# A quarter of the tokens leaves the dense expert products of a product-key layer: gathered rows and VectorE in their place

## The chip, the cores and the metric

One core of a Trainium2 chip runs the whole program in one launch. The metric is device microseconds of that core, as the median of the runs shown. TensorE (PE) multiplies, with weight loads (PEld) beside the products; VectorE (DVE), ScalarE (ACT) and GpSimd (POOL) work element by element; SyncE (SP) issues most transfers, GpSimd some.

## The reference

256 tokens of width 2048 pass a first block (a convolution and a state-space branch, then a product-key expert layer) and then two more layers. The change lies in the expert layer. Each token picks 16 experts for each of 8 heads out of 128 x 128 = 16384; expert e is a row of `u_tab` and a row of `v_tab`, both of 2048 numbers.

```python
def peer(h, w_q, sub_keys, u_tab, v_tab):
    """h: (B,S,D) -> (B,S,D). Product-key retrieval of single-neuron experts."""
    bsz, seq, d = h.shape
    tokens = h.reshape(bsz * seq // PEER_TOKEN_BLOCK, PEER_TOKEN_BLOCK, d)

    def block(xb):
        q = (xb @ w_q).reshape(PEER_TOKEN_BLOCK, PEER_HEADS, 2, PEER_HALF)
        s = jnp.einsum('thcd,hcnd->thcn', q, sub_keys).astype(jnp.float32)
        s_top, i_top = lax.top_k(s, PEER_TOPK)
        cand = s_top[:, :, 0, :, None] + s_top[:, :, 1, None, :]
        cand_idx = i_top[:, :, 0, :, None] * PEER_KEYS + i_top[:, :, 1, None, :]
        cand = cand.reshape(PEER_TOKEN_BLOCK, PEER_HEADS, PEER_TOPK * PEER_TOPK)
        cand_idx = cand_idx.reshape(PEER_TOKEN_BLOCK, PEER_HEADS, PEER_TOPK * PEER_TOPK)
        best, pos = lax.top_k(cand, PEER_TOPK)
        expert = jnp.take_along_axis(cand_idx, pos, axis=-1)
        gates = jax.nn.softmax(best, axis=-1).astype(xb.dtype)
        u_sel = u_tab[expert]
        v_sel = v_tab[expert]
        act = jax.nn.gelu(jnp.einsum('td,thkd->thk', xb, u_sel))
        return jnp.einsum('thk,thkd->td', gates * act, v_sel)

    out = lax.map(block, tokens)
    return out.reshape(bsz, seq, d)
```

The rest of the program (convolution, scan, gated delta rule, band attention, the large projections) keeps its operations.

## The kernel before

All data is float32. A product on TensorE runs in two or three passes on rounded parts: a number is split into a high part (`h`) and the rest (`l`). For every strip of weights, `strips` fetches a `raw` tile of 128 x 1024 by SP (`fetch`, L150), ScalarE makes its high part (`wh`, L162) and VectorE the rest (`wl`, L163), both into a ring that holds two such tiles; `raw` has three buffers. `self.width` says how many columns one L162 or L163 instruction takes: 1024 in the first block up to the experts, 512 from the experts to the end of the program.

The expert layer is computed densely, without looking which experts were picked.

- **`experts_in`.** After the queries (16 products with `peer_w_q`), 128 blocks follow, one for each 128 experts (the number c). A block has two `raw` tiles, thus 16 pieces of the contraction; for each piece `dual` issues a matmul of 512 columns (L175: `wh` times high and low part of 256 tokens) and one of 256 (L176: `wl` times the high part). `fold` (L181, L182) adds the two halves, L797 scales, and gelu goes to the activations `w` on ScalarE (L801, L803).
- **Top-k and gates.** During blocks 0 to 31 VectorE finds the picks (`topk`, two steps a block). After block 31 `gates` turns each token's picks into a 128 x 128 gate matrix: three VectorE instructions per token (`oj`, L942 and L944), two small matmuls (L954), and for eight tokens at a time a product into `w` (L966, L968). `GRATE` sets how many steps of it are issued in a piece of the contraction.
- **`experts_out`.** For each pair of experts c, c+1 and each of four groups of 512 output columns (first three groups, then the last), the activations are split (`ah`, `al`, L1009, L1010) and multiplied with a strip of `peer_v`: per expert three matmuls of 512 columns for each half of the tokens, six in all (L1018 to L1020). `finish` transposes the sums, adds the residual and hands on.

The program is written with generators (`Side`) whose steps are spread over the loops; a scheduler then orders each engine's instructions, by priorities and its own estimates. What stands in the built program is fixed: an engine takes its instructions in that order, and an instruction that waits holds up all behind it.

## Time and profile before

| | before |
|---|---|
| runs | 3355.83 us median of 3 (3353.45 to 3359.02) |
| profiled execution | 3351.08 us, span 3349.3 us |
| busy in the span | PE 3291.0, DVE 2667.1, ACT 2021.3, POOL 171.6 us |
| moved by DMA | 584.49 MB, mean 175 GB/s |
| granted TensorE clock, mean | 0.996 |

A row of a view names the line, the engine, the operation, and output and inputs by the program's names with their shapes (partitions x elements). The modelled length of a matmul runs over the start of the next, so the pace of TensorE is read from starts, not from lengths. VectorE's instructions overlap a little as well: what one costs behind another is the distance of their starts.

### The profile page before, as it was taken

The numbers are of one execution on the slowest core, as the hardware profiler recorded it, in microseconds if no ns is written. First come the engines' busy times: TensorE is split into PE (matmuls) and PEld (weight loads), VectorE is DVE, ScalarE is ACT, GpSimd is POOL, SyncE is SP. The second block draws the span as 40 slices with busy tenths as digits, with TensorE's granted clock in tenths as the row PEclk, the third lists the DMA queues.
The fourth block names the chain that finished last, engine by engine and source line by source line (L and its number), as shares of the span: only waits on it lengthen the run. The fifth ranks groups of instructions, "written<-read, shape, count | busy, mean of one in ns | idle before, by whom it ended". The sixth has DMA issues, their size and how long they took to land.

```text
span 3349.3 us, 53879 instructions
## 1 busy us (share of the span) xinstructions
PE 3291.0 (98%) x17962; PEld 2780.5 (83%) x17962; DVE 2667.1 (80%) x6200; ACT 2021.3 (60%) x4529; POOL 171.6 (5%) x319
## 2 busy tenths in 40 slices
PE   8999999999999999999999999999999999999999
PEld 7787778888888888888888888778888888888888
DVE  8999987789999999996555556868888768666685
ACT  6577755555555555555555556767666666566664
POOL 1211110000000000000000000000222100000000
PEclk9999999999999999999999999999999999999999
DMA  6544345765556555555666666655443436655556
GB/s 210 160 143 139 133 127 188 216 193 178 187 183 179 180 177 182 177 182 183 193 194 195 193 192 198 209 183 171 143 138 117 145 105 211 198 177 176 173 171 181
DMA packets 167655, 584.49 MB, mean 175 GB/s; under 512 B 19184, under 2 KB 25616, under 8 KB 167120
## 3 DMA queue, kind: packets, MB, share of 16 engines
q1 hardware_dynamic: 165600, 574.94, 54.8%
q0 software_dynamic: 1776, 6.10, 0.6%
q8 instruction: 141, 2.31, 0.3%
q14 instruction: 138, 1.13, 0.1%
HBM read 573.88 MB, written 7.09 MB: 173 GB/s over the span
## 4 chain that ended last, share of the span: by engine, by line
PE 90%; DVE 5%; ACT 2%; issue 1%; DMA 1%; POOL 1%; SPq 0%; ACTq 0%; DVEq 0%; POOLq 0%
PE g L175 36%; PE g L176 18%; PE va L1018 7%; PE va L1019 7%; PE va L1020 7%; PE g L1609 3%; PE g L1610 3%; PE g L1608 3%; DVE wl L163 2%; PE ip L1345 1%; ACT wh L162 1%; PE yp L639 1%; PE wp L954 1%; PE cps L175 1%; PE bu L611 1%
## 5 line engine op out<-in xcount | busy, mean ns | idle before, releaser
L162 ACT CAST wh<-raw 128x512 fp32r<-128x512 f32 (+1 forms) x1920 | 1274.2, 664 | 1080.3 <-PE g L175 553.2
L163 DVE TENSOR_TENSOR wl<-raw,wh 128x512 fp32r<-128x512 f32 (+1 forms) x1920 | 1433.8, 748 | 589.6 <-ACT wh L162 571.8
L175 PE MATMUL g<-X,wh 128*128 128x512 f32 x4752 | 1707.7, 401 | 23.0 <-ACT wh L162 8.8
L176 PE MATMUL g<-X,wl 128*128 128x256 f32 x4752 | 1337.0, 281 | 2.3 <-DVE wl L163 2.2
L175 PEld LDWEIGHTS g<-X,wh 128*128 128x128 f32 x4752 | 894.3, 188 | 234.6 <-issue 10.8
L176 PEld LDWEIGHTS g<-X,wl 128*128 128x128 f32 x4752 | 898.0, 189 | 9.9 <-DVE wl L163 5.1
L1018 PE MATMUL va<-wh,ah 128*128 128x512 f32 x1024 | 398.4, 391 | 4.5 <-DVE gg L797 2.3
L1019 PE MATMUL va<-wh,al 128*128 128x512 f32 x1024 | 400.2, 391 | 0.3 <-DVE al L1010 0.3
L1020 PE MATMUL va<-wl,ah 128*128 128x512 f32 x1024 | 399.1, 390 | 0.0
L1018 PEld LDWEIGHTS va<-wh,ah 128*128 128x128 f32 x1024 | 191.7, 188 | 46.9 <-ACT ah L1009 7.5
L1019 PEld LDWEIGHTS va<-wh,al 128*128 128x128 f32 x1024 | 192.6, 188 | 43.3 <-DVE al L1010 3.3
L1020 PEld LDWEIGHTS va<-wl,ah 128*128 128x128 f32 x1024 | 192.7, 188 | 39.7
L175 PE MATMUL g<-xo,wh 128*128 128x512 f32 x512 | 179.6, 395 | 0.0
L182 DVE TENSOR_TENSOR g<-g,fold 128x256 f32<-128x256 f32 x377 | 159.8, 424 | 4.5 <-ACT fold L181 4.0
L1608 PE MATMUL g<-wh,X 128*128 128x512 f32 x384 | 151.9, 396 | 0.0
L1610 PE MATMUL g<-wl,X 128*128 128x512 f32 x384 | 150.5, 392 | 0.0
L1609 PE MATMUL g<-wh,X 128*128 128x512 f32 x384 | 150.1, 391 | 0.0
L181 ACT COPY fold<-g 128x256 f32<-128x256 f32 x377 | 138.2, 367 | 13.5 <-DVE g L182 7.7
L176 PE MATMUL g<-xo,wl 128*128 128x256 f32 x512 | 143.6, 280 | 0.0
L944 DVE TENSOR_SCALAR oj<-iota,ijg 128x128 f16<-128x128 f16 x512 | 142.6, 307 | 0.0
L175 PEld LDWEIGHTS g<-xo,wh 128*128 128x128 f32 x512 | 96.0, 187 | 22.8 <-DVE xo L1471 0.3
L1010 DVE TENSOR_TENSOR al<-w,ah 128x256 fp32r<-128x256 f32 x256 | 106.7, 418 | 0.9 <-ACT ah L1009 0.8
(478 smaller groups left out, 3577.0 us busy)
## 6 DMA issues: line engine op xcount, KB each, us to landing
raw<-peer_u SPq DMA_DIRECT2D x256, 512.0 KB, 3.5
raw<-peer_v SPq DMA_DIRECT2D x256, 512.0 KB, 3.5
raw<-a_w_in SPq DMA_DIRECT2D x128, 512.0 KB, 3.5
raw<-w_in SPq DMA_DIRECT2D x112, 512.0 KB, 3.5
raw<-b_w_t SPq DMA_DIRECT2D x96, 512.0 KB, 3.5
raw<-w_out SPq DMA_DIRECT2D x32, 512.0 KB, 4.3
raw<-peer_w_q SPq DMA_DIRECT2D x32, 512.0 KB, 3.5
raw<-a_w_out SPq DMA_DIRECT2D x32, 512.0 KB, 3.7
```

What stands on the lines that cost most here:

```text
L162: self.marks["A"] = nc.scalar.copy(wh[:, e], raw[:, e])
L163: self.marks["V"] = nc.vector.tensor_tensor(out=wl[:, e], in0=raw[:, e], in1=wh[:, e].bitcast(F32), op=ALU.subtract)
L175: nc.tensor.matmul(pf, lhsT=wh, rhs=hl, start=start, stop=False)
L176: return nc.tensor.matmul(pf[:, :T], lhsT=wl, rhs=hl[:, 0], start=False, stop=stop)
L182: self.nc.vector.tensor_tensor(out=pf[:, :T], in0=pf[:, :T], in1=t, op=ALU.add)
L944: V.tensor_scalar(out=oj[:, k, :], in0=iota, scalar1=ijg[:, 1, t : t + 1], scalar2=ijg[:, 2 + k, t : t + 1], op0=ALU.is_equal, op1=ALU.mult)
L1018: nc.tensor.matmul(ps, lhsT=ah, rhs=wh, start=first, stop=False)
L1019: nc.tensor.matmul(ps, lhsT=al, rhs=wh, start=False, stop=False)
L1020: nc.tensor.matmul(ps, lhsT=ah, rhs=wl, start=False, stop=last)
L1608: nc.tensor.matmul(ps[a], lhsT=xh[:, k, s], rhs=wh, start=k == 0, stop=False)
L1609: nc.tensor.matmul(ps[a], lhsT=xl[:, k, s], rhs=wh, start=False, stop=False)
L1610: self.marks["P"] = nc.tensor.matmul(ps[a], lhsT=xh[:, k, s], rhs=wl, start=False, stop=k == KT - 1)
```

## The change

The last S = 64 of the 256 tokens no longer take part in the dense products. N = 192 tokens do.

- `dual` issues matmuls of 384 and 192 columns for the 128 blocks of `experts_in`; `fold`, L797, gelu, `oj` and the gate products shrink to 192 tokens. The query products keep 256.
- In `experts_out` a strip's second group of three matmuls becomes two: one of 512 columns whose weights hold 64 high and 64 low parts (`bhl`), one with 64 weights (`bh`). ScalarE copies twice for it (192 and 64 columns); the split is one VectorE instruction of 192.
- The 64 tokens have 64 x 8 x 16 = 8192 picks: 64 gathers of 128 rows. Partition p of 64 tokens x 2 holds a token's heads in two halves. `rows` lays out the 64 tokens by token (two VectorE instructions of 2048, 16 transposes); `take` computes the expert numbers and moves them and the gates across partitions by GpSimd DMAs.
- `dots`: for each of 64 picks, an indirect DMA issued by GpSimd brings 128 rows of `peer_u` (2048 numbers, 1 MB), and VectorE multiplies and sums them with the tokens in one instruction (L191 of the changed kernel, with a second small one that writes the sum). `sums`: for each pick again 128 rows of `peer_v`, once 1536 numbers wide (`v_a`, 0.79 MB) and once 512 (`v_b`, 0.26 MB), scaled and added by one VectorE instruction (L206, L208).
- `stream` has two buffers: gather c+2 is issued when pick c has been used.
- `self.width` stays 1024 for the rest of the program, and the pool `em` has 7 larger buffers for 8.

```diff
-GRATE = 0.2
+GRATE = 0.08
...
+S = 64
+N = T - S
+NW = 8192 // N
+USTEP = 2.0 / 3.0
...
+        self.buf = [hb[:, 2048 * i : 2048 * i + 2048] for i in range(2)]
+        k.nc.gpsimd.tensor_tensor(out=self.sel, in0=k.ident[:, :S], in1=k.ident[:, S:], op=ALU.add)
...
+    def rows(self, x, rstd):
+
+        k, nc = self.k, self.k.nc
+        xs = self.buf[0].rearrange("p (k i t) -> p k i t", k=KT, i=2)
+        h, l = (v.bitcast(F32)[:, :, N:].unsqueeze(2).to_broadcast([P, KT, 2, S]) for v in x)
+        nc.vector.tensor_tensor(out=xs, in0=h, in1=l, op=ALU.add)
+        r = rstd[:, N:].unsqueeze(1).unsqueeze(1).to_broadcast([P, KT, 2, S])
+        nc.vector.tensor_tensor(out=xs, in0=xs, in1=r, op=ALU.mult)
+        xs = xs.rearrange("p k i t -> p k (i t)")
+        for q in range(4):
+            ps = k.ips.tile([P, 512], F32, name="xt", tag="i")
+            for i in range(4):
+                nc.tensor.transpose(ps[:, i * P : i * P + P], xs[:, 4 * q + i, :], k.ident)
+            nc.scalar.copy(self.acc[:, 512 * q : 512 * q + 512], ps)
...
+    def take(self, ij, gate, e, u, g):
+
+        nc = self.k.nc
+        V = nc.vector
+        V.scalar_tensor_tensor(out=e, in0=ij[:, 0, :], scalar=float(P), in1=ij[:, 1, :], op0=ALU.mult, op1=ALU.add)
+        u = u.bitcast(U32)
+        V.tensor_copy(u, e)
+        V.tensor_scalar(out=g, in0=gate, scalar1=GATE, scalar2=None, op0=ALU.mult)
+        for q in range(2):
+            s = slice(S * q, S * q + S)
+            nc.gpsimd.dma_start(self.idx[s], u[S:, s])
+            nc.gpsimd.dma_start(self.gate[s], g[S:, s])
+
+    def gather(self, table, c, w):
+        b = self.buf[c % 2][:, :w]
+        off = bass.IndirectOffsetOnAxis(ap=self.idx[:, c : c + 1], axis=0)
+        self.k.nc.gpsimd.indirect_dma_start(out=b, out_offset=None, in_=table, in_offset=off)
+        return b
+
+    def stream(self, table, w, use):
+        bufs = [self.gather(table, c, w) for c in range(2)]
+        yield
+        for c in range(S):
+            use(c, bufs[c % 2])
+            if c + 2 < S:
+                self.gather(table, c + 2, w)
+            yield
+
+    def dots(self):
+        nc = self.k.nc
+        V = nc.vector
+
+        def use(c, b):
+            V.tensor_tensor_reduce(out=b, in0=b, in1=self.acc, scale=1.0, scalar=0.0, op0=ALU.mult, op1=ALU.add, accum_out=self.h[:, c : c + 1])
+            if c % 16 == 15:
+                s = slice(c - 15, c + 1)
+                nc.scalar.activation(self.co[:, s], self.h[:, s], AF.Gelu_apprx_tanh)
+                V.tensor_tensor(out=self.co[:, s], in0=self.co[:, s], in1=self.gate[:, s], op=ALU.mult)
+
+        yield from self.stream(self.k.I["u_rows"], 2048, use)
+
+    def sums(self, table, o, w):
+        V = self.k.nc.vector
+        acc = self.acc[:, o : o + w]
+
+        def use(c, b):
+            s = self.co[:, c : c + 1]
+            if c == 0:
+                V.tensor_scalar(out=acc, in0=b, scalar1=s, scalar2=None, op0=ALU.mult)
+            else:
+                V.scalar_tensor_tensor(out=acc, in0=b, scalar=s, in1=acc, op0=ALU.mult, op1=ALU.add)
+
+        yield from self.stream(table, w, use)
...
-        nc.tensor.matmul(pf, lhsT=wh, rhs=hl, start=start, stop=False)
-        return nc.tensor.matmul(pf[:, :T], lhsT=wl, rhs=hl[:, 0], start=False, stop=stop)
...
+        n = hl.shape[2]
+        nc.tensor.matmul(pf[:, : 2 * n], lhsT=wh, rhs=hl, start=start, stop=False)
+        return nc.tensor.matmul(pf[:, :n], lhsT=wl, rhs=hl[:, 0], start=False, stop=stop)
...
-                self.width = W2
-                self.em = Tmp(E(tc.tile_pool(name="em", bufs=8)))
+                self.em = Tmp(E(tc.tile_pool(name="em", bufs=7)))
...
+                if k == 1:
+                    self.picks.rows(x, rstd)
...
+            tokens, sparse = Side(), Side()
             self.gated = 0
 
             for c in range(P):
                 self.block = c
-                ps = self.gemm([I["peer_u"][c, 0], I["peer_u"][c, 1]], x, self.mix((tokens, GRATE, "")))
-                g = sm.tile([P, T], F32, name="gg")
-                V.tensor_tensor(out=g, in0=ps, in1=rstd, op=ALU.mult)
+                ps = self.gemm([I["peer_u"][c, 0], I["peer_u"][c, 1]], x, self.mix((tokens, GRATE, ""), (sparse, USTEP / 16, "")), N)
+                g = sm.tile([P, N], F32, name="gg")
+                V.tensor_tensor(out=g, in0=ps, in1=rstd[:, :N], op=ALU.mult)
+                if c == 31:
+                    side.drain()
+                    w += [self.big_tile(f"w{k}")[:, : NW * N].rearrange("p (c t) -> p c t", t=N) for k in (1, 2)]
+                    w.append(self.picks.rest)
+                    tokens.add(self.gates(wps, ijg, iota16, w))
+                    sparse.add(self.picks.dots())
...
+            self.picks.take(ij[:, :, 1, :], ex.rearrange("p g k -> p (g k)")[:, P:], area(P), area(P), area(P))
...
+                sparse.add(picks.sums(I["v_a" if g0 == 0 else "v_b"], 512 * g0, 512 * ng))
...
-                        ah = self.em.tile([P, T], F32R, name=f"ah{e}")
-                        al = self.em.tile([P, T], F32R, name=f"al{e}")
+                        pa = self.em.tile([P, 2 * N + S], F32R, name=f"pa{e}")
                         with tc.high_priority(None):
-                            nc.scalar.copy(ah, a)
-                            V.tensor_tensor(out=al, in0=a, in1=ah.bitcast(F32), op=ALU.subtract)
-                        parts.append((ah, al))
+                            nc.scalar.copy(pa[:, :N], a)
+                            nc.scalar.copy(pa[:, N:T], a[:, :S])
+                            V.tensor_tensor(out=pa[:, T:], in0=a, in1=pa[:, :N].bitcast(F32), op=ALU.subtract)
+                        parts.append((pa[:, S:N], pa[:, T + S :], pa[:, N:T], pa[:, N : T + S]))
...
+                            ah, al, bh, bhl = parts[e]
                             first, last = c + e == 0, c + e == P - 1
-                            for a in range(2):
-                                ah, al = (x[:, a * P : a * P + P] for x in parts[e])
-                                ps = acc[g][a]
-                                nc.tensor.matmul(ps, lhsT=ah, rhs=wh, start=first, stop=False)
-                                nc.tensor.matmul(ps, lhsT=al, rhs=wh, start=False, stop=False)
-                                nc.tensor.matmul(ps, lhsT=ah, rhs=wl, start=False, stop=last)
+                            a, b = acc[g]
+                            nc.tensor.matmul(a, lhsT=ah, rhs=wh, start=first, stop=False)
+                            nc.tensor.matmul(a, lhsT=al, rhs=wh, start=False, stop=False)
+                            nc.tensor.matmul(a, lhsT=ah, rhs=wl, start=False, stop=last)
+                            if last:
+                                nc.tensor.matmul(b[:S], lhsT=bh, rhs=wl, start=False, stop=False)
+                            nc.tensor.matmul(b, lhsT=bhl, rhs=wh, start=first, stop=last)
+                            if not last:
+                                nc.tensor.matmul(b[:S], lhsT=bh, rhs=wl, start=False, stop=False)
                     side.step()
+                    sparse.step()
...
+    A["u_rows"] = np.ascontiguousarray(g["peer_u"][0])
+    A["v_a"] = np.ascontiguousarray(g["peer_v"][0][:, :1536])
+    A["v_b"] = np.ascontiguousarray(g["peer_v"][0][:, 1536:])
```

How this moves VectorE's order is seen at three places. The first is a block of `experts_in` in the gate part. Before, around block 50, four `wl` of 512 columns share it with the gates' `oj` (L942, L944), `fold` (L182), the scaling (L797) and the product with gelu (L804):

```order
1714 L163 TENSOR_TENSOR wl<-raw,wh 128x512
1715 L182 TENSOR_TENSOR g<-g,fold 128x256
1716 L944 TENSOR_SCALAR oj<-iota_6624,ijg 128x128
1717 L797 TENSOR_TENSOR gg<-g,rstd_6618 128x256
1718 L163 TENSOR_TENSOR wl<-raw,wh 128x512
1719 L942 TENSOR_SCALAR oj<-iota_6624,ijg 128x128
1720 L804 TENSOR_TENSOR w_9460<-w_9460,gg 128x48
1721 L944 TENSOR_SCALAR oj<-iota_6624,ijg 128x128
1722 L163 TENSOR_TENSOR wl<-raw,wh 128x512
```

In the changed kernel, around block 65, `wl` is L259, `fold` L279, the scaling L898, the product with gelu L911, `oj` L1050 and L1052; `ISA sb,sa` is the dot over 2048 numbers, `ISA sa` writes its sum:

```order
1824 L259 TENSOR_TENSOR wl<-raw,wh 128x1024
1825 L279 TENSOR_TENSOR g<-g,fold 128x192
1826 L191 ISA sb,sa<-sb,sa 128x2048
1827 L191 ISA sa 128x1
1828 L259 TENSOR_TENSOR wl<-raw,wh 128x1024
1829 L898 TENSOR_TENSOR gg<-g,rstd_6617 128x192
1830 L1050 TENSOR_SCALAR oj<-iota_6623,sa 128x128
1831 L1052 TENSOR_SCALAR oj<-iota_6623,sa 128x128 x2
1832 L911 TENSOR_TENSOR w_9302<-w_9302,gg 128x64
1833 L1050 TENSOR_SCALAR oj<-iota_6623,sa 128x128
1834 L1052 TENSOR_SCALAR oj<-iota_6623,sa 128x128 x2
1835 L191 ISA sb,sa<-sb,sa 128x2048
```

Two dots stand in one block, where the loop's step of `USTEP` would issue two in three blocks. All 64 stand between the scalings of blocks 30 and 67, so in 37 blocks.

The second place is VectorE around block 72, where the first group of `sums` (L208, 1536 wide) stands:

```order
1914 L259 TENSOR_TENSOR wl<-raw,wh 128x1024
1915 L279 TENSOR_TENSOR g<-g,fold 128x192
1916 L898 TENSOR_TENSOR gg<-g,rstd_6617 128x192
1917 L1050 TENSOR_SCALAR oj<-iota_6623,sa 128x128
1918 L1052 TENSOR_SCALAR oj<-iota_6623,sa 128x128 x2
1919 L259 TENSOR_TENSOR wl<-raw,wh 128x1024
1920 L911 TENSOR_TENSOR w_9302<-w_9302,gg 128x80
1921 L1050 TENSOR_SCALAR oj<-iota_6623,sa 128x128
1922 L1052 TENSOR_SCALAR oj<-iota_6623,sa 128x128 x2
1923 L208 SCALAR_TENSOR_TENSOR sa<-sb,sa 128x1536 x2
```

They were issued in `experts_out` and now stand in `experts_in`: all 64 of them between blocks 68 and 98, two in a block.

The third is VectorE around block 104, with the narrow group of `sums`:

```order
2308 L208 SCALAR_TENSOR_TENSOR sa<-sb,sa 128x512
2309 L259 TENSOR_TENSOR wl<-raw,wh 128x1024
2310 L208 SCALAR_TENSOR_TENSOR sa<-sb,sa 128x512 x2
2311 L259 TENSOR_TENSOR wl<-raw,wh 128x1024
2312 L279 TENSOR_TENSOR g<-g,fold 128x192
```

These 64 end at block 115, three or four in a block. VectorE's order in `experts_out` holds none of the 192 gathered instructions; there stand `wl`, the split and `finish`.

## Rows read from the trace of the kernel before

**Rows 1.** The page's part 1: busy time, share, instructions.
```profile
PE 3291.0 (98%) x17962; PEld 2780.5 (83%) x17962; DVE 2667.1 (80%) x6200; ACT 2021.3 (60%) x4529; POOL 171.6 (5%) x319
```

**Rows 2.** Busy time per engine in stretches; then TensorE clock, DMA share, GB/s.
```profile
1000.00:1200.00 200.00, 200.00 (x1281) 175.07 (x1280) 186.21 (x553) 117.24 (x284) 0.00 (x0) 1.00 0.59 179
...
1700.00:1900.00 200.00, 200.00 (x884) 165.58 (x884) 118.55 (x198) 106.92 (x197) 0.00 (x0) 1.00 0.61 193
2060.00:2235.00 175.00, 172.51 (x756) 138.21 (x755) 139.90 (x284) 131.21 (x298) 2.82 (x10) 1.00 0.65 203
```

**Rows 3.** DMA issues of both tables: ns, first and last start.
```profile
L150 SPq DMA_DIRECT2D raw<-peer_u x256: 327/328/328, 776.9 to 1521.9; - x128
```
```profile
L150 SPq DMA_DIRECT2D raw<-peer_v x256: 327/328/400, 1524.7 to 2232.0; - x128
```

**Rows 4.** TensorE in order of time at 1100 us: start, length, instruction.
```profile
1099.84 0.40 PE L175 MATMUL g<-X,wh 128*128 128x512 f32 x1
1100.07 0.28 PE L176 MATMUL g<-X,wl 128*128 128x256 f32 x1
1100.18 0.39 PE L175 MATMUL g<-X,wh 128*128 128x512 f32 x1
```

**Rows 5.** VectorE in order of time, in the top-k part of `experts_in`.
```profile
944.33 1.21 DVE L910 TENSOR_REDUCE btk<-btk 128x64 f32<-128x1024 f32 x1
945.46 1.45 DVE L163 TENSOR_TENSOR wl<-raw,wh 128x512 fp32r<-128x512 f32 x2
...
949.65 0.42 DVE L797 TENSOR_TENSOR gg<-g,rstd 128x256 f32<-128x256 f32 x1
949.98 1.22 DVE L903 TENSOR_TENSOR btk<-btk,iota 128x1024 f32<-128x1024 f32 x1
```

**Rows 6.** VectorE in order of time, in the gate part of `experts_in`.
```profile
1300.07 0.31 DVE L944 TENSOR_SCALAR oj<-iota,ijg 128x128 f16<-128x128 f16 x1
1300.29 0.31 DVE L942 TENSOR_SCALAR oj<-iota,ijg 128x128 bf16<-128x128 f16 x1
```

**Rows 7.** VectorE by line and shape, whole run: count, busy us, mean ns, idle.
```profile
L163 DVE TENSOR_TENSOR wl<-raw,wh 128x1024 fp32r<-128x1024 f32 x192 | 238.5, 1242 | 66.4 <-ACT wh L162 66.1
...
L1010 DVE TENSOR_TENSOR al<-w,ah 128x256 fp32r<-128x256 f32 x256 | 106.7, 418 | 0.9 <-ACT ah L1009 0.8
...
L486 DVE SCALAR_TENSOR_TENSOR X<-x,vecs,X 128x256 fp32r<-128x256 f32 x32 | 15.4, 481 | 0.0
...
L1309 DVE TENSOR_REDUCE tab<-tab 128x128 f32<-128x1024 f32 x4 | 7.7, 1931 | 0.0
...
L997 DVE SCALAR_TENSOR_TENSOR x1r<-va,x1r 128x512 f32<-128x512 f32 x8 | 5.5, 687 | 3.2 <-DMA x1r<-x1d 1.9 <-PE va L1020 0.8 <-PE va L995 0.4
```

**Rows 8.** ScalarE by line and shape, whole run.
```profile
L162 ACT CAST wh<-raw 128x1024 fp32r<-128x1024 f32 x192 | 201.0, 1047 | 161.6 <-PE g L175 147.0 <-issue 13.8
...
L1009 ACT CAST ah<-w 128x256 fp32r<-128x256 f32 x256 | 101.7, 400 | 0.0
```

**Rows 9.** DMA issues: count, KB each, median us from issue to landing.
```profile
raw<-peer_u SPq DMA_DIRECT2D x256, 512.0 KB, 3.5
...
rep<-gd POOLq DMA_DIRECT2D x1, 2048.0 KB, 10.0
bias<-b_bias POOLq DMA_DIRECT2D x16, 128.0 KB, 3.3
...
bs<-sub_keys SPq DMA_DIRECT2D x1, 1024.0 KB, 5.6
```

**Rows 10.** GpSimd's own time for issuing a DMA, by line.
```profile
L1336 POOL DMA_DIRECT2D tab<-xdr x4 | 4.8, 1194 | 2.6 <-DMA xdr<-tab 2.4
```

**Rows 11.** Three stretches, columns as in rows 2.
```profile
600.00:690.00 90.00, 89.98 (x518) 78.85 (x517) 64.44 (x99) 50.05 (x82) 0.00 (x0) 1.00 0.74 225
2248.00:2256.00 8.00, 2.69 (x9) 1.87 (x10) 4.28 (x11) 4.71 (x14) 0.00 (x0) 0.64 0.44 150
8.00:10.00 2.00, 1.54 (x4) 0.93 (x5) 2.00 (x4) 2.00 (x6) 0.00 (x0) 1.00 1.03 404
```

110 lines of the change are left out of this document (64 added, 46 removed).

## The prediction

> **What bounds the kernel now.** The page's shares come first: TensorE 98%, VectorE 80%, ScalarE 60% [rows 1]. These are averages, so the expert stage is read by itself. The issues of `peer_u` start at 776.9 us and those of `peer_v` at 1524.7 us and end at 2232.0 us [rows 3]: `experts_in` takes 747.8 us, `experts_out` 707.3 us. In order of time the 512-column matmul is followed after 0.23 us and the 256-column one after 0.11 us [rows 4], so one piece takes 0.345 us, 0.449 ns per column, and weight loads add nothing. 128 blocks of 16 pieces are 707 us, which with the gates' matmuls fills `experts_in`; 3072 matmuls of 0.23 us are 706.6 us, which fills `experts_out`. TensorE bounds both. But the reader should look at the column beside it: in `experts_in` VectorE is busy 186.2 of 200 us, in `experts_out` 118.6 of 200, and 139.9 of 175 in its last part [rows 2]. The first has nothing to give, the second much.
>
> **TensorE's part.** A piece of `experts_in` falls to 576 columns, 0.259 us, and a block to 4.14 us (5.52 before). If a 192-column matmul (0.086 us) cannot cover the next weight load, the block grows: a load was covered by 0.11 us [rows 4], so at most 0.03 us a piece, 4.6 us a block. `experts_out` falls from six to five matmuls a strip, 2560 x 0.23 = 589 us, **-118 us**.
>
> **VectorE's costs.** From starts that follow each other: 256 columns 0.33 us (949.65 to 949.98), 1024 columns 1.13 us (944.33 to 945.46) [rows 5], so 1.04 ns per element and 0.07 us. A `wl` of 1024 lasts 1242 ns and costs about 1.155 us; an `oj` 0.22 us [rows 6]; 192 columns 0.27 us. No row has 2048 columns: the dot comes to 2.20 us, its small second instruction to 0.08 us, together 2.28 us. Nothing in the rows is faster per element; from above, the reduction of L1309 needed 1931 ns for 1024 columns [rows 7], so 3.8 us for a dot. I take 2.28, as all other rows of two inputs follow that line. `scalar_tensor_tensor` with 512 columns lasts 687 ns, like `tensor_tensor`; with a scalar from memory a 256-column one lasts 481 against 418 ns [rows 7], so 0.05 us more: 1.70 us for 1536, 0.63 us for 512. All picks: 64 x (2.28 + 1.70 + 0.63) = 295 us, and the order puts every one of them into `experts_in`.
>
> **`experts_in`, block by block.** A block in the gate part costs VectorE: two `wl` 2.31, `fold` and scaling 0.54, six `oj` (two tokens) 1.35, gelu product about 0.17, gate products about 0.19 (a quarter of 650 elements, estimated), sum 4.56 us. That is already what TensorE needs. With the picks, by the order:
> - blocks 31 to 67: 37 x 4.56 + 64 x 2.28 = 315 us;
> - 68 to 97: 30 x 4.56 + 64 x 1.70 = 246 us;
> - 98 to 115: 18 x 4.56 + 64 x 0.63 = 122 us;
> - the last 12: 55 us.
>
> Blocks before them have two `wl` (2.31), `fold` and scaling (0.54) and two 1024-column instructions (2.26), 5.1 us; a block was 5.65 us (944.33 to 949.98 [rows 5]). With waits for ScalarE I take 5.3, 32 x 5.3 = 170 us. Total 908 us against 747.8: **+160 us**. Where TensorE had pace to gain, VectorE now sets it.
>
> **The gathers.** Each dot or sum stands in VectorE's queue and waits there for its gather; behind it wait `wl` and so TensorE. A gather starts when the pick two before is done, so a pick takes at least half of (gather + its own time + about 0.1). From GpSimd 128 KB landed after 3.3 us and 2048 KB after 10.0 us [rows 9], on a line 6.4, 5.5 and 3.75 us for the three widths. The row numbers must be read and 128 descriptors built, for which no row stands; a plain issue took GpSimd up to 1.19 us [rows 10], and I add 0.8 us: 7.2, 6.3, 4.55 us. Per pick: (7.2 + 2.4) / 2 = 4.8 us where VectorE needs 315 / 64 = 4.9, no wait; (6.3 + 1.8) / 2 = 4.05 against 3.84, 13 us; (4.55 + 0.73) / 2 = 2.64 against 1.91, 47 us. The picks are not evenly spaced (two stand side by side, then a block's work), for which I add 40 us: **+100 us**. Lower bound 0; upper, each gather also waits behind a strip's landing, 3.5 us [rows 9]: some 380 us. Bandwidth alone isn't the limit: a block of dots moves 1.05 + 1.73 x 1.05 MB in 8.5 us, 337 GB/s, and 404 GB/s were moved at the start [rows 11].
>
> The Trainium skill ("DMA: Bandwidth & Descriptors", Anatomy of one DMA) gives a GpSimd-issued transfer about 2.0 us plus its bytes at 436 GB/s. An estimate by that page is 4.4, 3.8 and 2.6 us for the gathers, all hidden, and 100 us less in the sum. The 2048 KB row speaks against it: 10.0 us, where the page gives 6.8.
>
> **The rest.** The first gather waits for `take`'s moves, about 3 us, and itself: of 10 us some 8 stay (**+8**). `rows` is two 2048-column instructions, 4.5 us, and 16 transposes: **+6**. In `experts_out` ScalarE has, for each pair of experts in the last part, one `wh` (1047 ns) and four copies, some 1.83 us, and the 20 us of `finish` that its 131.2 us [rows 2] hold beyond `wh` and `ah` [rows 8]; 137 of TensorE's 147 us. The ring's halves leave half a microsecond of room, so I allow **+15 us** of stalls for both parts. The width of 1024 in the last 1100 us: TensorE was at 89.98 of 90 us with it [rows 11], so 0, within ±15. TensorE will work half the time in 85 blocks; where it worked 2.7 of 8 us its granted clock read 0.64 [rows 11]. At the lower level (1.2 GHz) a block is 8.3 us, near VectorE's own 8.5, 8.2 and 6.8 us, so this costs at most about 30 us; I take **+10**.
>
> **Sum.** 3351.1 (the profiled execution) + 160 + 100 + 8 + 6 + 10 - 118 + 15 = 3532 us. The median stands 4.7 us above the profiled execution: **3537 us**, 5% slower.
>
> **Rivals.**
> - *The gathers are hidden.* VectorE alone then sets 908 us, and the sum is 3437 us. For it: the first two periods are close to VectorE's own. Against: the narrow gathers.
> - *The gathers come later.* With 1.5 us more each, the periods become 5.55, 4.8 and 3.4 us, 240 us of waits with the uneven spacing instead of 100: 3677 us; with 3 us more 3820. The mechanism: GpSimd must build descriptors while VectorE runs one instruction of two inputs after the other. The Trainium skill ("SBUF — State Buffer", Who interferes with whom) says that such an instruction keeps GpSimd from reading SBUF until it ends. No row here shows GpSimd reading indices, so this stays open.
> - *Faster.* One mechanism: VectorE's pick instructions run at two elements per cycle. Then they cost 148 us instead of 295; `experts_in` takes 761 us, no wait remains, and the time is 3290 us. It decides where the picks cost less than some 200 us in all, waits included. Against it: no two-input float32 row is below 1.04 ns per element.
> - *The changes cancel*: the picks cost about 200 us, within 0.2% of before.
> - *A slow dot* of 3.8 us adds up to 97 us, 3634 us.
>
> **How the numbers follow.** Forecast with waits of 40 to 220 us: 0.53. Hidden gathers 0.17. Late gathers 0.16, slow dot 0.03. Faster 0.08, no change 0.03. Slower by over 0.2% (about what a measurement of this kernel can tell) then has 0.89. The range takes in the hidden gathers, with 15 us for the width, and ends where the later gathers begin: 3420 to 3665 us, leaving about 0.2 outside.
>
> **What the profile would show.** Right: in `experts_in` VectorE busy or waiting for DMA all the time, TensorE at about half between the blocks 31 and 115 and waiting for `wl`; dots of 2.3 us; the stage near 1020 us; `experts_out` near 600 us; and many VectorE waits that end with the landing of `sb`, most in the narrow group. Wrong, if the dots are far from 2.3 us, if the gathers land far from 7, 6 and 4.5 us, or if `experts_out` does not fall to about 600 us because half-size room in the ring stalls it.

## The result: 3632.9 us, 8.2% slower

Before: 3357.4 us (median of 4 runs, 3353.5 to 3360.7). After: 3632.9 us (4 runs, 3622.3 to 3636.7). The ratio is 1.0816, 95% interval 1.0790 to 1.0842. The forecast was 3537 us with a range of 3420 to 3665 us: the sign and the range hold the result, and the likeliest value is 96 us too low.

The profile of the changed kernel begins with the shares that answer to [rows 1], and further down its page has TensorE's granted clock in 40 slices:

```profile
span 3634.9 us, 50084 instructions
...
PE 3239.2 (89%) x17386; PEld 2743.5 (75%) x17386; DVE 2781.1 (77%) x5366; ACT 1879.9 (52%) x3901; POOL 456.7 (13%) x516
...
PEclk9999999999978888887799999999999999999999
```

No engine stands at its limit over the span any more; TensorE fell from 98 to 89%. The span divides by the DMA issues, as [rows 3] did before:

```profile
L246 SPq DMA_DIRECT2D raw<-peer_u x256: 327/328/328, 780.3 to 1887.2; - x128
L246 SPq DMA_DIRECT2D raw<-peer_v x256: 327/328/395, 1890.4 to 2509.2; - x128
```

The stage of `peer_u` (first issue of `peer_u` to first of `peer_v`) went from 747.8 to 1110.1 us, +362.3. That of `peer_v` (first to last issue) went from 707.3 to 618.8 us, -88.5. What lies behind the last issue grew by 8.4 us and what lies ahead of the first by 3.4. The loss lies in the first stage, so it is cut by what its blocks carry: the first 32 blocks, those with dots, with sums of 1536, with sums of 512, and the last ones (busy time of each engine, granted clock, DMA share, GB/s; to be read against [rows 2]):

```profile
core 0: us, PE busy (x) PEld busy (x) DVE busy (x) ACT busy (x) POOL busy (x), PEclk, DMA share, GB/s
780.30:973.20 192.90, 168.38 (x1096) 158.88 (x1094) 172.86 (x422) 91.86 (x140) 2.32 (x4) 0.99 0.58 184
973.20:1327.90 354.70, 238.40 (x1313) 217.44 (x1313) 303.55 (x551) 104.94 (x216) 103.90 (x64) 0.83 0.80 297
1327.90:1628.60 300.70, 198.48 (x1104) 185.88 (x1104) 253.74 (x423) 85.96 (x171) 95.05 (x65) 0.82 0.75 273
1628.60:1834.00 205.40, 129.40 (x625) 118.03 (x626) 130.53 (x277) 47.66 (x99) 81.55 (x64) 0.76 0.52 174
1834.00:1890.40 56.40, 52.64 (x368) 50.10 (x368) 48.49 (x113) 27.51 (x54) 0.00 (x0) 0.97 0.59 187
sum 1110.10, PE 787.30 PEld 730.33 DVE 909.18 ACT 357.94 POOL 282.82; mean PE 157.46 PEld 146.07 DVE 181.84 ACT 71.59 POOL 56.56
```

The last row is the one to read first: VectorE is busy 909.2 us in the stage; the prediction had worked out 908. (Its parts fit less well; more on that below.) The stage is 201 us longer than that, and the waits of VectorE in the same stretch (us in total, times, longest) name them:

```profile
DVE sa L208 <- DMA sb<-v_b,sa: 73.0, 28, 5.4
DVE sb L191 <- DMA sb<-u_rows,sa: 55.4, 32, 9.5
DVE sa L208 <- DMA sb<-v_a,sa: 44.7, 32, 3.7
DVE wl L259 <- ACT wh L258: 25.4, 31, 1.8
```

173 us are spent before landings of gathers, 9.5 of them before the first, where the sum had 108 (100 and the first gather's 8). 25 us are `wl` behind ScalarE, 19 of them in the first 32 blocks. What such a wait looks like in order of time on VectorE, in the narrow group, where it was worst:

```profile
1704.45 0.53 DVE L1052 TENSOR_SCALAR oj<-iota,sa 128x128 f16<-128x128 f16 x2
1707.98 0.75 DVE L208 SCALAR_TENSOR_TENSOR sa<-sb,sa 128x512 f32<-128x512 f32 x1 [3.00 <-DMA sb<-v_b,sa]
1708.65 1.22 DVE L259 TENSOR_TENSOR wl<-raw,wh 128x1024 fp32r<-128x1024 f32 x1
1709.79 0.75 DVE L208 SCALAR_TENSOR_TENSOR sa<-sb,sa 128x512 f32<-128x512 f32 x1
1714.22 0.75 DVE L208 SCALAR_TENSOR_TENSOR sa<-sb,sa 128x512 f32<-128x512 f32 x1 [3.69 <-DMA sb<-v_b,sa]
```

The `wl` at 1708.65 stands behind the sum that waited 3 us, and TensorE waits for that `wl`: between 973 and 1834 us it waited 288.6 us for `wl` in all.

The durations on which the sum stood, by line, engine and shapes, answer to [rows 7] and [rows 9]:

```profile
L191 DVE CUSTOM_DVE_ANT_0 sb<-sb,sa 128x2048 f32<-128x2048 f32 x64 | 146.8, 2294 | 55.4 <-DMA sb<-u_rows,sa 55.4
L208 DVE SCALAR_TENSOR_TENSOR sa<-sb,sa 128x1536 f32<-128x1536 f32 x63 | 114.5, 1818 | 45.0 <-DMA sb<-v_a,sa 44.7
...
L208 DVE SCALAR_TENSOR_TENSOR sa<-sb,sa 128x512 f32<-128x512 f32 x63 | 47.2, 750 | 73.2 <-DMA sb<-v_b,sa 73.0
```

```profile
sb<-u_rows,sa POOLq DMA_INDIRECT x64, 7.9
sb<-v_a,sa POOLq DMA_INDIRECT x64, 6.3
sb<-v_b,sa POOLq DMA_INDIRECT x64, 4.6
```

The dot lasts 2.29 us; from its start to that of VectorE's next instruction it is 2.22 (1138.19 to 1140.41 us; 2.28 was taken, its second instruction included). The gathers land after 7.9, 6.3 and 4.6 us (7.2, 6.3 and 4.55 were taken); the trace holds 16 of the 64 landings of each width.

### The profile page after: what moved, and what is told of

Read it like the earlier page. It is cut to its first block, busy times and chain, and to the rows that moved or that the text cites. A ratio compares the mean times of both kernels' runs of the same rounds, so it can differ in the third digit from the quotient of the medians.

```text
span 3634.9 us, 50084 instructions
## 1 busy us (share of the span) xinstructions
PE 3239.2 (89%) x17386; PEld 2743.5 (75%) x17386; DVE 2781.1 (77%) x5366; ACT 1879.9 (52%) x3901; POOL 456.7 (13%) x516
## 5 line engine op out<-in xcount | busy, mean ns | idle before, releaser
L272 PE MATMUL g<-X,wh 128*128 128x512 f32 (+1 forms) x4752 | 1705.8, 407 | 32.3 <-ACT wh L258 17.8
L259 DVE TENSOR_TENSOR wl<-raw,wh 128x1024 fp32r<-128x1024 f32 x1056 | 1299.5, 1231 | 559.5 <-ACT wh L258 551.1
L273 PE MATMUL g<-X,wl 128*128 128x256 f32 (+1 forms) x4752 | 1354.5, 285 | 321.2 <-DVE wl L259 320.8
L258 ACT CAST wh<-raw 128x1024 fp32r<-128x1024 f32 x1056 | 1108.1, 1050 | 945.4 <-PE g L272 456.4
L208 DVE SCALAR_TENSOR_TENSOR sa<-sb,sa 128x1536 f32<-128x1536 f32 (+1 forms) x126 | 161.8, 1284 | 118.2 <-DMA sb<-v_b,sa 73.0
L1127 PE MATMUL va<-wh,pa 128*128 128x512 f32 x512 | 202.1, 395 | 10.3 <-ACT pa L1118 6.3
L1128 PE MATMUL va<-wh,pa 128*128 128x512 f32 x512 | 204.8, 400 | 0.9 <-DVE pa L1120 0.9
L1129 PE MATMUL va<-wl,pa 128*128 128x512 f32 x512 | 203.2, 397 | 2.5 <-DVE wl L259 2.5
L1134 PE MATMUL va<-wl,pa 128*64 128x512 f32 x508 | 201.5, 397 | 0.0
L1132 PE MATMUL va<-wh,pa 128*128 128x512 f32 x512 | 199.9, 390 | 0.0
L191 DVE CUSTOM_DVE_ANT_0 sb<-sb,sa 128x2048 f32<-128x2048 f32 x64 | 146.8, 2294 | 55.4 <-DMA sb<-u_rows,sa 55.4
L279 DVE TENSOR_TENSOR g<-g,fold 128x256 f32<-128x256 f32 (+1 forms) x377 | 152.4, 404 | 3.6 <-ACT fold L278 3.4
```

The costliest lines, as they stand in the source:

```text
L258: self.marks["A"] = nc.scalar.copy(wh[:, e], raw[:, e])
L259: self.marks["V"] = nc.vector.tensor_tensor(out=wl[:, e], in0=raw[:, e], in1=wh[:, e].bitcast(F32), op=ALU.subtract)
L272: nc.tensor.matmul(pf[:, : 2 * n], lhsT=wh, rhs=hl, start=start, stop=False)
L273: return nc.tensor.matmul(pf[:, :n], lhsT=wl, rhs=hl[:, 0], start=False, stop=stop)
L1127: nc.tensor.matmul(a, lhsT=ah, rhs=wh, start=first, stop=False)
L1128: nc.tensor.matmul(a, lhsT=al, rhs=wh, start=False, stop=False)
```

## The experiments

Theory: the order puts all picks on VectorE's queue in a stage where VectorE had nothing to spare; its work and the waits of its in-order queue for gathers make the 362 us. Rivals: TensorE's lower clock sets the pace; transfers are the limit wherever the picks stand; the dense part itself does not gain. All times below are medians, each ratio is to the kernel before as measured beside that run (3354.5 to 3355.0 us; 3357.4 for the changed kernel); "stage u" and "stage v" are the two stretches defined above, in the profiled execution.

| kernel | us | ratio to before, 95% interval | stage u | stage v |
|---|---|---|---|---|
| before | 3357.4 | 1 | 747.8 | 707.3 |
| after | 3632.9 | 1.0816 (1.0790 to 1.0842) | 1110.1 | 618.8 |
| e1 no gathers in the loops | 3473.4 | 1.0354 (1.0337 to 1.0371) | 950.8 | 619.0 |
| e2 no picks | 3255.6 | 0.9705 (0.9689 to 0.9721) | 733.9 | 617.2 |
| e3 steps tied | 3465.1 | 1.0328 (1.0311 to 1.0345) | 809.9 | 732.2 |
| e4 eight narrow buffers | 3566.9 | 1.0631 (1.0609 to 1.0652) | 1040.1 | 616.3 |
| e5 no picks, splits of 512 | 3181.9 | 0.9483 (0.9467 to 0.9499) | 667.5 | 616.6 |
| e6 after, splits of 512 | 3569.0 | 1.0640 (1.0622 to 1.0658) | 1051.4 | 611.0 |
| e7 tied, 512, eight buffers | 3395.3 | 1.0118 (1.0101 to 1.0135) | 793.8 | 693.2 |
| e8 before, splits of 1024 | 3362.3 | 1.0024 (1.0015 to 1.0034) | 747.8 | 714.5 |
| e9 e7, GpSimd helps | 3390.6 | 1.0100 (1.0083 to 1.0117) | 792.9 | 694.3 |
| e10 gathers of 64 columns | 3548.0 | 1.0573 (1.0555 to 1.0591) | 1019.8 | 618.4 |
| e11 e7, strips in halves | 3317.4 | 0.9887 (0.9870 to 0.9903) | 779.4 | 629.4 |
| e12 e11, GpSimd helps | 3332.8 | 0.9929 (0.9912 to 0.9947) | 775.8 | 665.8 |

### e1: the waits for gathers

```diff
             use(c, bufs[c % 2])
-            if c + 2 < S:
-                self.gather(table, c + 2, w)
             yield
```

> Only the first two gathers of each table are issued; every dot and sum is still executed, in the same blocks, on the rows that these two brought. Left out: the rows of the other 62 picks of each table, so the last 64 tokens' expert sums are not the reference's. In the changed kernel VectorE stood 173 us before landings of the gathers. Theory (VectorE's in-order work plus waits for gathers sets the stage, and nothing else is as long): about 3633 - 170 = 3460 us, within 20, and the stage from the first issue of peer_u to the first of peer_v near 940 us. Rival 'TensorE's lower clock sets the pace': a block costs some 9 us at the lower level, 85 blocks 770 us instead of 861, about 3545 us. Rival 'the waits for gathers covered other waits that come back' (ScalarE's wh, raw pieces): 3560 us or more.

Measured 3473 us, the theory's figure within its margin. Only the waits for the first gathers of the three tables are left, 12.9 us (8.5 of them for the first of all, as the sum had it), so 160 us of waits went and 160 us of time: they had covered nothing else. (The order moved a little: the narrow sums end in block 110, not 115.) The stage's row in e1, and two of VectorE's waits in it:

```profile
782.70:1733.50 950.80, 733.46 (x4506) 682.08 (x4504) 902.85 (x1783) 357.06 (x677) 11.07 (x10) 0.91 0.46 147
```

```profile
DVE wl L257 <- ACT wh L256: 30.1, 37, 2.2
DVE sb L189 <- DMA sb<-u_rows,sa: 8.5, 1, 8.5
```

TensorE's granted clock in the blocks with picks was still only 0.90; the stage took 951 us, 48 us more than VectorE's 903 busy. Of these 13 are the first gathers, 30 `wl` behind ScalarE and 5 the rest, so the lower clock can have cost 35 us at most here. That rival had 3545 us and falls.

### e2 and e5: what the dense part gains

e2, and e5's edit on top of it:

```diff
-                    sparse.add(self.picks.dots())
...
-                sparse.add(picks.sums(I["v_a" if g0 == 0 else "v_b"], 512 * g0, 512 * ng))
```

```diff
+                self.width = W2
                 self.em = Tmp(E(tc.tile_pool(name="em", bufs=7)))
```

> No gather, no dot and no sum is issued; the dense products on 192 tokens and all else stay. Left out: the expert sums of the last 64 tokens. Theory: blocks 31 to 127 fall back to what VectorE and TensorE need without picks, about 4.6 us each, 97 x 4.6 = 446 us instead of 914, and the time is about 3633 - 468 = 3165 us. If the 192-column matmul does not cover the weight load fully, the same 4.6 us a block. Rival 'the dense part itself became slower' (the half-size room in the ring, the lower clock): blocks of 5.5 us and more, 3250 us or above. The stage of peer_v shows its 619 us again if picks have no part in it.

Measured 3256 us, the rival's figure. Stage u shrank by 14 us to 733.9, although TensorE's columns had fallen by a quarter. A stretch of its blocks shows neither engine full, and ScalarE waiting for TensorE's last use of a half of the ring:

```profile
1100.00:1300.00 200.00, 181.69 (x1236) 172.41 (x1235) 162.05 (x395) 97.26 (x198) 0.00 (x0) 0.96 0.57 179
```

```profile
ACT wh L258 <- PE g L272: 25.1, 21, 3.0
```

So the half-size room in the ring was tested by itself:

> As e2 (no gather, dot or sum; the expert sums of the last 64 tokens are left out), and the ring's splits stay 512 columns wide after the first part, as in the kernel before. It asks why e2 gained only 14 us in the stage of peer_u, where 75 were expected. Theory (a split of 1024 columns fills half the ring at once: wh 1.05 us and wl 1.24 us one after the other are as long as TensorE's 2.3 us on the other half, so VectorE's other work shows as a stall): with finer splits a block comes to about 5.0 us (16 pieces of 0.285 us and the gates' matmuls) instead of 5.6, the first 32 blocks lose 10 us too, the stage of peer_v 10 to 15 us and the rest 8 us: about 3170 us. Rival 'the piece of 0.285 us and VectorE's order set the block, whatever the split': 3235 us or more, only the rest and the first blocks gain.

Measured 3182 us, the theory's figure within 12 us. Blocks of 16 pieces of 0.285 us and the gates' matmuls now fill TensorE, 463.8 of 476 us, and 80 us of stage u are gained:

```profile
970.00:1446.00 476.00, 463.76 (x3343) 445.74 (x3342) 445.39 (x1258) 279.08 (x705) 0.00 (x0) 1.00 0.66 205
```

The 0.285 us itself is near the bound that the prediction gave for a weight load that a 192-column matmul can't cover (0.03 us a piece). TensorE at full clock in e2, in order of time (PEld is a weight load):

```profile
1200.15 0.19 PEld L272 LDWEIGHTS g<-X,wh 128*128 128x128 f32 x1
1200.24 0.36 PE L272 MATMUL g<-X,wh 128*128 128x384 f32 x1
1200.26 0.19 PEld L273 LDWEIGHTS g<-X,wl 128*128 128x128 f32 x1
1200.43 0.25 PE L273 MATMUL g<-X,wl 128*128 128x192 f32 x1
1200.52 0.36 PE L272 MATMUL g<-X,wh 128*128 128x384 f32 x1
```

From the 192-column start to the next it is 0.09 us, from the 384-column start 0.19 (0.199 in median in e5), where 384 x 0.449 ns are 0.17. The loss stands behind the longer matmul: its successor's weight load starts 0.11 us after the load before it, and so 0.02 us after the 384-column matmul has begun. In the kernel before, the same load and the 512-column matmul began together (both at 1099.84 us).

### e8 and e6: the split's width by itself

e8 is one line of the kernel before (its `self.width = W2` ahead of the expert stage is left out); e6 is the line of e5 on the changed kernel.

> The kernel before with one line changed: splits of 1024 columns everywhere; nothing left out. Theory: TensorE's half of the ring lasts 2.76 us there, wh and wl 2.5 us, so stalls appear where VectorE is busy 0.9 of the time: 30 to 60 us in the stage of peer_u, nothing in that of peer_v, 8 us in the rest: about 3405 us. Rival 'the width costs nothing where TensorE is the bound': 3355 to 3365 us.

Measured 3362 us, 0.24% slower, and stage u did not change: TensorE has not one wait in its profile between 1000 and 1500 us. The theory was wrong, the rival right. With 5.52 us a block TensorE spends 2.76 us on a half of the ring, and `wh` and `wl` of the next half (1.05 and 1.24 us, one after the other) fit in with 0.47 us to spare. After the change it spends 2.28 us: nothing is left for VectorE's other work. In stage u the width costs only together with the shorter matmuls; e8's few microseconds are in stage v (707.3 to 714.5).

> The changed kernel with splits of 512 columns after the first part, as before the change; nothing left out. Theory (where picks stand VectorE itself is the limit, so the split's width matters only outside them): first 32 blocks 12 us, last blocks 10, stage of peer_v 15, rest 8 us less: 3590 us. Rival 'the coarse ring is what makes the waits for picks show': 100 us less or more, 3530 us. Rival 'twice as many splits only add their fixed cost on VectorE': 3640 us.

Measured 3569 us, 64 us less, between theory and rival; 59 us of it are in stage u. By the start of each block's scaling (L898, in e6 L899), 13 of these are in blocks 0 to 30, where the theory had 12, and 44 in blocks 31 to 119, where it had only the last blocks' 10: most of that is the rival's. VectorE's waits for gathers fell from 173 to 120 us and those of `wl` for ScalarE from 25 to 6.5; the picks stand a little later in the order (the last in block 119, not 115). One reason is on GpSimd. Its own time for a gather of `u_rows` fell with the width (min, median, max in ns); first the changed kernel, then e6:

```profile
L174 POOL DMA_INDIRECT sb<-u_rows,sa x64: 939/1682/1947, 973.2 to 1320.7; - x64
```

```profile
L174 POOL DMA_INDIRECT sb<-u_rows,sa x64: 936/1145/1149, 960.5 to 1306.8; - x64
```

It can't be the only one: for `v_b` the median rose from 951 to 1120 ns, and its waits fell all the same, from 73 to 55 us.

### e4 and e10: what a gather's time is made of

e4 gives the 512-column gathers eight buffers in the room of the two (and starts eight ahead):

```diff
+    def ring(self, w):
+        if w > 512:
+            return [b[:, :w] for b in self.buf]
+        return [b[:, o : o + w] for b in self.buf for o in range(0, 2048, w)]
...
-            use(c, bufs[c % 2])
-            if c + 2 < S:
-                self.gather(table, c + 2, w)
+            use(c, bufs[c % n])
+            if c + n < S:
+                self.gather(table, c + n, w)
```

> The gathers of 512 columns use eight buffers in the same room instead of two; all else stays. Nothing is left out. Theory (a gather restarts only when the pick two before is done, so latency is shown): the 73 us of waits in the narrow group fall to about 10, time about 3633 - 60 = 3573 us. Rival 'GpSimd or the transfers themselves are the limit there': the waits stay above 50 us, 3615 us or more. Rival 'the lower clock of TensorE (0.76 in that stretch) sets the floor': 18 blocks of 9.1 us are 164 us against 205, 3595 us.

Measured 3567 us: the waits of the narrow group went to nothing (the sums of 1536 and the dots kept 47.0 and 50.8), and with 75 us of waits 66 us of time. GpSimd and the transfers delivered the narrow rows fast enough; two buffers were too few for a gather of 4.6 us beside a sum of 0.75.

```diff
     def gather(self, table, c, w):
-        b = self.buf[c % 2][:, :w]
+        b = self.buf[c % 2][:, : w if c < 2 else 64]
...
-            use(c, bufs[c % 2])
+            use(c, self.buf[c % 2][:, :w])
```

> The changed kernel, but from the third gather of each table on only 64 columns of each row are brought (32 KB instead of 1 MB, 0.75 MB and 0.25 MB); dots and sums keep their widths and places and work on what the buffers hold. Left out: the rest of the rows, so the last 64 tokens' expert sums are not the reference's. It asks whether the waits come from bytes or from what every gather needs whatever its size. Theory (each gather is some 4 us plus its bytes at about 270 GB/s, by 7.9, 6.3 and 4.6 us for the three sizes): a small gather lands after 3.5 to 4 us, the waits of the dots and of the sums of 1536 go, half of those in the narrow group stay: 3633 - 140 = 3495 us. Rival 'the fixed part is GpSimd kept waiting by VectorE': landings of 5 us and more, 3550 us or above. Rival 'all is bytes': landings under 2.5 us and the time of e1, 3473 us.

Measured 3548 us, the figure of the rival 'fixed part'. The landings of these small gathers are not in the profile, but VectorE's waits are, 86 us in all:

```profile
DVE sa L208 <- DMA sb<-v_b,sa: 60.6, 24, 4.8
DVE sb L191 <- DMA sb<-u_rows,sa: 14.4, 7, 7.0
DVE sa L208 <- DMA sb<-v_a,sa: 10.7, 12, 2.0
```

So the waits of the large gathers come from bytes (100 to 25 us), those of the narrow group hardly (73 to 61): there the part that every gather needs is longer than what VectorE does meanwhile. Where VectorE waited, it took 4.6 to 4.7 us (median in each group, first two gathers left out) from a gather's start to the start of its dot or sum, between the theory's 3.5 to 4 and the rival's 5. GpSimd's own time is 1.1 to 1.7 us of that (medians), so that VectorE holds GpSimd up can be a part of the fixed part and not the whole; what the rest is was not tested.

### e3 and e7: the picks at the places that the source gives them

```diff
-                ps = self.gemm([I["peer_u"][c, 0], I["peer_u"][c, 1]], x, self.mix((tokens, GRATE, ""), (sparse, USTEP / 16, "")), N)
+                ps = self.gemm([I["peer_u"][c, 0], I["peer_u"][c, 1]], x, self.mix((tokens, GRATE, ""), (sparse, USTEP / 16, "V")), N)
...
-                    sparse.step()
+                    sparse.step(1, (self, "V"))
```

With it the order has one dot in one and a half blocks over almost all of 32 to 127 and the sums between the strips of `peer_v`.

> Each step of the picks is tied behind the newest wl split on VectorE, so that the order keeps the place that the source gives it: one dot per one and a half blocks in blocks 32 to 127, the sums one per pair of experts in the stage of peer_v. Nothing is left out. Theory (the place of the picks on VectorE's queue is the cause): a block needs 4.56 + 0.667 x 2.37 = 6.1 us, 97 blocks 595 us instead of 914; gathers lie 9 us apart with two buffers, so no wait; the sums of 1536 fit under TensorE's 6.9 us a pair, those of 512 add 10 to 30 us in the last part: about 3633 - 319 + 25 = 3340 us. Rival 'gathers land too late wherever they are' (contention or a blocked GpSimd): 1 to 2 us remain for each of 192 picks, 3500 us. Rival 'TensorE's lower clock sets the pace': TensorE is busy 3/4 of a block, its clock falls, 9.1 us a block, 3600 us.

Measured 3465 us: 168 us better than after, 125 worse than expected. In stage u the theory holds: 809.9 us (788 expected), one wait of 5.1 us for a gather, a clock of 0.98. Stage v missed: 732 us instead of some 645. DMA was at 0.83 to 0.86 of its time there, and ScalarE stood 140 us before raw strips that had not landed. VectorE's wait for a dot in stage u, and ScalarE's for strips from 1592 to 2100 us:

```profile
DVE sb L191 <- DMA sb<-u_rows,sa: 5.1, 1, 5.1
```

```profile
ACT wh L258 <- DMA raw<-peer_v: 128.7, 46, 5.8
```

> The steps tied as in e3, splits of 512 columns, and eight buffers for the gathers of 512 columns; nothing left out. Theory: the costs that e3 left are the coarse ring (12 us in the first blocks, 15 in the blocks with dots, 40 in the stage of peer_v, 10 in the rest) and 41 us of waits for the narrow gathers, of which 30 go: 3465 - 107 = 3358 us, the time of the kernel before. Rival 'the transfers of gathers and strips collide' (ScalarE stood 140 us before late raw strips in e3's stage of peer_v): that part stays, 3400 us or more.

Measured 3395 us, 37 above the theory's figure and 5 below the rival's bound. VectorE waits 2.7 us for gathers in both stages, but ScalarE still waits for strips, in the blocks (980 to 1565 us) and in stage v (1580 to 2020 us):

```profile
ACT wh L265 <- DMA raw<-peer_u: 110.5, 58, 4.7
```

```profile
ACT wh L265 <- DMA raw<-peer_v: 130.1, 54, 5.4
```

A strip is fetched when one of three buffers is free, which is after VectorE's last split of it. A dot of 2.3 us ahead of that split makes the next strip late.

### e9, e11 and e12: what is left

e9 moves two instructions to GpSimd; e11 (of its edit the lines of the split) fetches strips in halves into six half buffers, in the same room; e12 is both.

```diff
-                    V.tensor_tensor(out=d[:, :n], in0=d[:, :n], in1=g[:, :n], op=ALU.mult)
+                    nc.gpsimd.tensor_tensor(out=d[:, :n], in0=d[:, :n], in1=g[:, :n], op=ALU.mult)
...
-                            V.tensor_tensor(out=pa[:, T:], in0=a, in1=pa[:, :N].bitcast(F32), op=ALU.subtract)
+                            (nc.gpsimd if g0 and e else V).tensor_tensor(out=pa[:, T:], in0=a, in1=pa[:, :N].bitcast(F32), op=ALU.subtract)
```

```diff
+            r = raw[:, e] if whole or src.space != DRAM else self.fetch(src[:, e])
             with self.tc.high_priority(None):
-                self.marks["A"] = nc.scalar.copy(wh[:, e], raw[:, e])
+                self.marks["A"] = nc.scalar.copy(wh[:, e], r)
```

> e7, and two small VectorE instructions of two inputs go to GpSimd: the product of gelu and gate in the blocks of the stage of peer_u, and in the last part of the stage of peer_v the 192-column subtraction of every second expert. Nothing is left out. Theory (VectorE's busy time is what the picks cost where TensorE is not the limit): 97 blocks lose 0.25 us each, 64 pairs 0.35 us each with the waits behind them: 3395 - 24 - 35 = 3336 us, 0.5% below the kernel before. Rival 'GpSimd is held up by VectorE's instructions and holds them up': its gathers come later and nothing is gained, 3395 us or more. Rival 'transfers are the limit' (0.77 to 0.89 of the DMA engines' time): 3380 us or more.

Measured 3391 us, 5 us better than e7, so the theory fails. The rival 'transfers' stays; the other had 3395 us or more and is missed by 4 us. VectorE's busy time between 970 and 1575 us fell from 583.1 to 576.8 us, where the moved products had lasted 22.

> e7, and where splits are 512 columns wide a strip is fetched in two halves of 256 KB into six half buffers in the room of the three strips, each free again after its own split. Nothing is left out. In e7 ScalarE stood 110 us in the blocks and 130 us in the first part of the stage of peer_v before late raw strips, since a strip's buffer is free only after VectorE's last split of it and VectorE works off a dot or sum in between. Theory (the three strip buffers behind VectorE's queue are what is left of e7's loss): half of that comes back as time, 30 us in the blocks and 15 in the stage of peer_v: 3395 - 45 = 3350 us, level with the kernel before. Rival 'the transfers themselves are the limit' (0.77 to 0.89 of the DMA engines' time): 3385 us or more, and with halves of 2 KB per row not better. Rival 'VectorE's busy time is the limit in the blocks' (583 of 605 us): 3375 to 3390 us.

Measured 3317 us, 78 us better than e7 and 1.1% below the kernel before (ratio 0.9887, interval 0.9870 to 0.9903): the theory's direction, and more than its size. The place is another: 64 us of it are in stage v and 14 in stage u, where the theory had 15 and 30. ScalarE's wait for strips fell to 32 us (980 to 1500 us) and 71 us (1560 to 2000 us). The rival 'transfers' falls, since they now run faster, 333 GB/s at 0.95 of the DMA engines' time (e7 had 301 at 0.89), and TensorE is full beside them:

```profile
1550.00:1980.00 430.00, 420.98 (x1853) 324.28 (x1853) 376.72 (x568) 262.15 (x617) 68.72 (x61) 0.99 0.95 333
```

In the blocks VectorE is now the limit, 518.4 of 530 us; its rival had 3375 to 3390 us and falls by the number, since the gain came in the other stage:

```profile
970.00:1500.00 530.00, 453.13 (x2994) 414.70 (x2994) 518.43 (x1248) 248.12 (x636) 63.26 (x56) 0.97 0.78 275
```

A half strip is free earlier, and it is also a smaller transfer; no run takes the two apart.

> e11 with the two edits of e9 (the gate product and every second subtraction of the last part on GpSimd). Nothing is left out. Theory: with late strips out of the way VectorE's busy time is the limit of a block, so taking 0.25 us a block from it now shows: 25 to 40 us below e11, near 3315 us. Rival 'transfers': the same time as e11 within 5 us. Rival 'VectorE and GpSimd hold each other up' (in e9 VectorE's busy time in the blocks fell by 6 us where the moved products had lasted 22): within 10 us of e11.

Measured 3333 us, 15 us worse than e11: none of the three. Stage u gained 4 us, stage v lost 36, and what lies behind the last issue shrank by 12. A subtraction of 192 columns takes GpSimd 788 ns and VectorE 352. Among TensorE's waits between 1990 and 2200 us, 25 us in all where e11 has 16, there are now some for such results:

```profile
PE va L1146 <- DVE wl L275: 10.8, 25, 1.7
...
PE va L1145 <- POOL pa L1137: 4.6, 4, 2.2
```

That is 9 us of the 36; where the others went is not settled.

## Why the prediction was right, and 96 us low

- **VectorE's work.** 908 us were worked out for stage u from starts that follow each other; the profile has 909.2. That it is so close is partly luck: the five parts were 170, 315, 246, 122 and 55 us, the rows above have 172.9, 303.6, 253.7, 130.5 and 48.5, and the misses cancel. Block 31 is counted twice in it (5 us), and the 170 held some waits. From starts that follow each other in the stretch above, a narrow sum costs 0.67 us (0.63 taken) and a `wl` 1.14 (1.155). This term, +160, stands, and e1 and e3 show that it is the place of the picks in the order that makes it count.
- **The gathers** are the term that was mis-sized: 108 us in the sum, 173 measured, and e1 shows that 160 of them were time. The step that failed is the mean period by which landings were turned into waits. By it the dots needed no wait at all; they took 46 us beyond the first. An estimate from the trace tells why: VectorE's instructions in their recorded order and with their own times, each gather issued when the pick two before is done. With the landings as predicted, evenly spaced picks would wait 52 us and the recorded order 106, so uneven spacing is worth some 54 us, not 40. With the landings as measured (7.9, 6.3, 4.6 us) and the measured 0.28 us from a pick's end to the next gather's start (0.1 taken) it is 139 us. The other 25 of the 164 us behind the first are left to the spread of the landings (5.6 to 10.2 us for `u_rows`), which no run separates. How spacing works is seen above: after two picks with only a `wl` between them (1707.98 and 1709.79 us) the next wait is 3.69 us, and the room that a gather has elsewhere doesn't make up for it.
- **The ring.** The prediction allowed for its halves in `experts_out` alone. In stage u the waits for ScalarE (25 us) had no term, but for what the 5.3 us a block of the first 32 held; those blocks took 193 us instead of 170. e5 against e2 shows 66 us where picks don't hide it.
- **The dense part.** The bound of 0.03 us a piece for weight loads came true (0.285 us for 0.259); behind VectorE it cost nothing here. Of stage v's -118 us, 88.5 came; the 15 us for stalls were 29. They are there without picks too (617 us in e2 and e5). TensorE's waits are 13 of them; the rest is its pace, 0.235 us from start to start where it was 0.229 before. What the split's width has in them is not clear: e6 has 8 us less than the changed kernel, e5 1 us less than e2.
- **The rest** grew by 8.4 us (1117.3 to 1125.7 behind the last issue), within the 15 allowed, and not by the split's width, for which the 15 stood: e6 has most of the growth without the width (1124.5), e8 the width without the growth (1118.5). Its cause was not tested.
- **The clock** fell to 0.76 to 0.83 in the blocks with picks, as forecast; TensorE was busy there for 63 to 67% of the time, where about half was expected. e1 leaves the clock 35 us at most; 10 were taken, and no run separates more.
- **Rivals.** 'Gathers hidden' had 3437 us; e1, where they are absent, gives 3473; 19 of the 36 us lie in stage u, where `wl` waits 30 us for ScalarE, and 15 in stage v. 'Gathers later' had 240 us of waits where the forecast had 100, and 173 lie between them. Its mechanism shows, at half the size assumed: GpSimd's own time for a gather of `u_rows` has a median 0.74 us above its least, not 1.5, and follows VectorE's splits (below). A slow dot and two elements a cycle are excluded by 2.29 us.

Put together from the runs, stage u went 747.8, -80 for the dense part (e5), +66 for the coarse ring (e2), +217 for the picks' instructions (e1), +159 for the gathers' waits (after): 1110 us. The sizes hold for this sequence; with the picks in place the coarse ring is worth 59 us (e6).

## What to carry to other kernels

Before work is moved off the busiest engine, look at the engine that would take it in the same stage, and at where the order will put it: the same instructions cost 275 us more than before as they stood and gained 37 us when tied to the splits, with the finer splits, eight narrow buffers and strips released in halves. (The kernel before was not run with half strips; its TensorE was busy 200 of 200 us in both stages [rows 2].) Behind an in-order queue a microsecond of wait for a gather was close to a microsecond of time (160 for 160 in e1, 66 for 75 in e4, 85 for 87 in e10), so count waits pick by pick and give small gathers more buffers before more bandwidth. When one side of a double buffer becomes shorter, work out again whether the other side still fits behind it: the 1024-column split was almost free before (e8) and cost 66 us in stage u after the matmuls had shrunk (e2 against e5).
